# First three tiles' products over features without the token's factor, with their inputs loaded alternately

## The chip, the cores and the metric

The kernel runs on one core of one Trainium2 chip. The metric is the device time of one execution in microseconds (us); the median of three runs of the kernel before is 988.71. The core has five engines that work side by side, each through a queue of its own and in that queue's order: TensorE (PE) for matrix products into PSUM, VectorE (DVE), ScalarE (ACT), GpSimd (POOL), and SyncE (SP), which here only issues DMAs.

## The reference

One inference step of a decoder layer, over 512 prompt tokens and 8 samples of 8 tokens, 1024 features each. The start of it is what matters here:

```python
mod = jnp.matmul(cs, P['ada_w'][l]) + P['ada_b'][l]          # cs = silu(c)
sh1, sc1, g1, sh2, sc2, g2 = split(mod, 6)
hn = rmsnorm(x, P['norm1_w'][l]) * (1.0 + sc1) + sh1
u = jnp.matmul(hn, P['w_in'][l])
z, xbc, dt_raw, q, k, v, o, ig, fg, xr, gr = jnp.split(u, ...)
xbc = silu(causal_conv(xbc, ...))
```

rmsnorm multiplies each token by one factor, 1/sqrt(mean(x*x) + eps), and each feature by a weight. The scale sc1 and the shift sh1 depend on the feature and on the group: one set for the prompt, one for each sample. Since the token's factor r is a number for each column, W(x * amp * r + sh) is (W(x * amp)) * r + W sh, with amp = weight * (1 + sc1). Behind the projection come three mixers (an SSD scan, an mLSTM, a gated recurrence), an output projection and an MLP.

## The kernel before

Features lie on the 128 partitions, tokens in the free dimension: x is eight tiles (k = 0 to 7) of 128 x 576, 512 prompt columns and 64 sample columns. A weight block is 128 outputs by 1024 inputs; there are 124 of them, and each product runs in three passes over split operands (high weight by high x, high by low, low by high), each pass in two halves of 288 columns (mm_k, lines 155 to 165). One block with its eight k is 48 matmuls. w_prep (lines 132 to 153) splits a block: ACT copies the high half into fp32r, DVE subtracts for the low half. Three raw blocks fit in SBUF at a time.

Two PSUM pairs (psg) rotate through the blocks, and four single banks (psm) serve everything else. A block's first matmul so waits until the block two before it has been read out.

start (lines 327 to 419) is written inside in_order, which makes every engine keep the order in which the code is written. It does, in this order:

- SP loads the eight x tiles, the small vectors (vec), then the adaLN weights in pairs (ada, q = 0 to 7, 1 MB each in four DMAs; a pair holds shift and scale of tile q) with the weight blocks between them.
- ACT and DVE square all x tiles, PE sums over features (sum_tokens), DVE and POOL make the token's factor (rstd_cols), PE and ACT spread it over the partitions (rstd_bcast: five transposes, two copies).
- For each k: ada_mm (PE, one pair's rows), ada_sel (PE selects, DVE adds the bias into modt), modulate (lines 285 to 302): DVE multiplies the prompt columns by amp and factor in place, POOL does the 64 sample columns in three small steps, ACT adds the shift into the high half hnh, DVE subtracts for the low half hnl, POOL subtracts for the samples' low half and adds the shift to x itself (line 301, for the gates).
- Between them mm_k for the first three blocks (conv channels 8, 10 and 0), by the table TODO: products of tile k follow as soon as hn[k] is there. The third block sits in two psm banks.
- gates_mm: the gate columns from the modulated x, copied and selected. ev_gates and ev_conv read the results out; conv (lines 604 to 635) copies a block's PSUM with three ACT instructions into a row buffer, and ACT, DVE and POOL go on from there.

From there run (line 1269) goes through block 4 and up by unit, two slots of side work (gate_rows, the scans, the adaLN of later stages) per block, ordered by the framework's scheduler.

Of the kernel before, what the change touches and what calls it, by code (L numbers as in the profile page):

```python
# [67 lines left out]
class Kernel:  # L68
# [53 lines left out]
    def w_load(self, upto):  # L122
        while self.w_next_dma <= min(upto, NBLK - 1):
            b = self.w_next_dma
            t = self.T("wg") if b == 0 else self.wpool.tile([128, 1024], FT, name=self.name("raw"), tag="raw", bufs=RAW_BUFS)
            src = self.io["wg"] if b == 0 else self.io["w"][b - 1]
            n = src.shape[1]
            self.nc.sync.dma_start(t[:, :n], src)
            self.w_raw[b] = t[:, :n].rearrange("p (k m) -> p k m", k=8)
            self.w_next_dma += 1  # L130

# [153 lines left out]
    def modulate(self, x, rb, k):  # L285

        nc = self.nc
        amp = self.rpool.tile([128, 9], FT, name=self.name("amp"), tag="amp", bufs=3)
        sc, sh = self.mod("sc1", k), self.mod("sh1", k)
        nc.vector.tensor_scalar(amp, sc, 1.0, self.v("nw1")[:, k:k + 1], op0=OP.add, op1=OP.mult)  # L290
        p, s = x[:, :TP], x[:, TP:].rearrange("p (b t) -> p b t", b=NB)
        nc.vector.scalar_tensor_tensor(p, p, amp[:, 0:1], rb[:, :TP], op0=OP.mult, op1=OP.mult)
        nc.gpsimd.tensor_tensor(x[:, TP:], x[:, TP:], rb[:, TP:], op=OP.mult)
        nc.gpsimd.tensor_tensor(s, s, amp[:, 1:, None].to_broadcast([128, NB, 8]), op=OP.mult)
        nc.gpsimd.tensor_tensor(s, s, sh[:, 1:, None].to_broadcast([128, NB, 8]), op=OP.add)
        hi, lo = self.T("hnh", FR), self.T("hnl", FR)
        nc.scalar.activation(hi[:, :TP], p, AF.Identity, bias=sh[:, 0:1])
        nc.scalar.activation(hi[:, TP:], x[:, TP:], AF.Copy)
        nc.vector.scalar_tensor_tensor(lo[:, :TP], p, sh[:, 0:1], hi[:, :TP].bitcast(FT), op0=OP.add, op1=OP.subtract)
        nc.gpsimd.tensor_tensor(lo[:, TP:], x[:, TP:], hi[:, TP:].bitcast(FT), op=OP.subtract)  # L300
        nc.gpsimd.tensor_scalar(p, p, sh[:, 0:1], None, op0=OP.add)
        return hi, lo

# [23 lines left out]
    def start(self):  # L327
# [6 lines left out]
        with self.in_order():  # L334
            x = [self.T("x") for _ in range(KT)]
            for k in range(KT):
                nc.sync.dma_start(x[k], io["x"][:, k])
# [10 lines left out]

            def load(q):
                ada[q] = [self.T("ada") for _ in range(4)]  # L350
                for i in range(4):
                    nc.sync.dma_start(ada[q][i][:, :512], io["ada"][q, :, i * 512:(i + 1) * 512])

            for q in range(PAIR_AT):
                load(q)
                self.w_load(W_AT.get(q, 0))
            ms = self.P("ms")
            self.warm(WARM[0])
            for k in range(0, KT, 2):
                sa, sb = self.R()[:, :NT], self.R()[:, :NT]  # L360
                nc.scalar.activation(sa, x[k], AF.Square)
                if k:
                    nc.vector.tensor_tensor(sb, x[k + 1], x[k + 1], op=OP.mult)
                else:
                    nc.scalar.activation(sb, x[k + 1], AF.Square)
                nc.vector.tensor_tensor(sb, sa, sb, op=OP.add)
                self.sum_tokens(sb, ms, k == 0, k == KT - 2)
                if k < KT - 2:
                    self.warm(WARM[1])
# [3 lines left out]
            r = self.rstd_cols(ms, 1.0 / D, EPS)  # L373
            rows = {}

            def ada_mm(q):
                t = ada.pop(q)
                rows[q] = self.ada_mm(lambda k: t[k // 2][:, (k % 2) * 256:(k % 2 + 1) * 256])

            ada_mm(0)  # L380
            self.w_prep(0)
            for q in range(PAIR_AT, KT):
                if q == VEC_AT:
                    nc.sync.dma_start(self.vec[:, NV1:], io["vec"][:, NV1:])
                load(q)
                self.w_load(W_AT.get(q, 0))
            self.w_load(4)
            self.start_dma = self.last()
            rb = self.rstd_bcast(r)
            self.warm(WARM[2])  # L390
            self.ada_sel(0, rows[0])
            self.hn = [None] * KT
            self.hn[0] = self.modulate(x[0], rb, 0)
            self.w_prep(1)
            self.warm(WARM[3])
            ada_mm(1)
            self.ada_sel(1, rows[1])
            ada_mm(2)
            pgs = [self.PG(), self.PG(), PairTile(banks=[self.P("g"), self.P("g")])]
            for k in range(KT):  # L400
                if k + 1 < KT:
                    self.hn[k + 1] = self.modulate(x[k + 1], rb, k + 1)
                if k in PREP_AT:
                    self.w_prep(2 + PREP_AT.index(k))
                if k == KT - 1 and GATES_FIRST:
                    ps = self.gates_mm(x)
                for n, (i, kk) in enumerate(TODO.get(k, [(0, k), (1, k), (2, k)])):
                    self.mm_k(pgs[i], 1 + i, kk, self.hn[kk], kk == 0, kk == KT - 1)
                    if n == 0:
                        if k + 2 < KT:  # L410
                            self.ada_sel(k + 2, rows[k + 2])
                        if k + 3 < KT:
                            ada_mm(k + 3)
            if not GATES_FIRST:
                ps = self.gates_mm(x)
            self.ev_gates(ps)
            self.ev_conv(pgs[0], 8)
        self.ev_conv(pgs[1], 10)
        self.ev_conv(pgs[2], 0)

    def gates_mm(self, x):
# [10 lines left out]
        nc.scalar.activation(g[:, HALF:], ps[1][:, :HALF], AF.Copy)  # L432
        for h in range(2):
            nc.tensor.matmul(ps[h][:96, :HALF], self.v("selg"), g[:, h * HALF:(h + 1) * HALF], start=True, stop=True)
        return ps
# [168 lines left out]
    def conv(self, pg, dst, wcols, bias, state, out):  # L604

        nc = self.nc
        r = self.R()
        nc.gpsimd.memset(r[:, 0:3], 0.0)
        nc.gpsimd.tensor_copy(r[:, 515:603].rearrange("p (b t) -> p b t", b=NB)[:, :, 0:3], state)
        nc.scalar.activation(r[:, 3:3 + HALF], pg.h[0][:, :HALF], AF.Copy)  # L610
        n = TP - HALF
        nc.scalar.activation(r[:, 3 + HALF:515], pg.h[1][:, :n], AF.Copy)
        nc.scalar.activation(r[:, 515:603].rearrange("p (b t) -> p b t", b=NB)[:, :, 3:11],  # L613
                             pg.h[1][:, n:HALF].rearrange("p (b t) -> p b t", b=NB), AF.Copy)
# [22 lines left out]
    def ev_conv(self, pg, i):  # L637

        nc = self.nc
        if not hasattr(self, "cso"):  # L640
# [6 lines left out]
                      self.v("cst")[:, 24 * i:24 * i + 24].rearrange("p (b t) -> p b t", b=NB), self.cso[:, i])  # L647
# [621 lines left out]
    def run(self):  # L1269
# [9 lines left out]
        blk = 4  # L1279
# [6 lines left out]
        for i in range(1, 4):  # L1286
            inp(lambda pg: self.ev_conv(pg, i))
# [180 lines left out]
WARM = 14, 4, 4, 6  # L1468
PAIR_AT = 3
W_AT = {0: 1, 2: 2, 4: 3}  # L1470
VEC_AT = 7
PREP_AT = 1, 3, 6
# [165 lines left out]
```

## Time and profile before

| | us |
|---|---|
| runs of the kernel before, median (lowest to highest) | 988.71 (987.87 to 989.5) |
| the profiled execution | 991.71 |
| its span in the trace | 989.9 |
| PE busy | 959.0 |
| DVE busy | 579.1 |
| ACT busy | 400.4 |
| POOL busy | 134.9 |

The profiled execution lies 3.0 us above the median, and 1.8 us of it are outside the span. A row of the timeline gives start, duration, engine, line, operation, what it writes <- what it reads, and in brackets how long the engine sat idle before it and what released it. Equal neighbours are merged (x2). An fp32r matmul of 288 columns has one record, an fp32 one two. Tiles are named without their buffer numbers; g is a block's PSUM, hnh and hnl the halves of the modulated x, wh, wl and wt those of a weight block, adap and adas the adaLN rows and their selection.

### The profile page before, as it was taken

To read this page: it belongs to the slowest core of one execution; us is meant where nothing else is said; L and a number is where in the kernel's file an instruction comes from. 1 tells how busy PE (TensorE), PEld (TensorE's weight loads), DVE (VectorE), ACT (ScalarE), POOL (GpSimd) and SP (SyncE) were. 2 spreads that over 40 slices of the span, in tenths; PEclk is the share of its full clock that TensorE was granted. 3 is DMA by queue.
4 is the path that set the end of the run, shared out by engine and by line. 5 is a ranking of instruction groups with operands and counts; after the bars stand their busy time and mean duration, and the time that the engine had idled before them with its cause. 6 is when DMAs were issued, how large, how long until landed. Compare 5 with 4: busy or idle time off the path is not lost.

```text
span 989.9 us, 18136 instructions
## 1 busy us (share of the span) xinstructions
PE 959.0 (97%) x7370; PEld 904.9 (91%) x7370; DVE 579.1 (59%) x1206; ACT 400.4 (40%) x741; POOL 134.9 (14%) x194
## 2 busy tenths in 40 slices
PE   8899879999899999999999999999999999999996
PEld 4789868888788889998999999999999999999996
DVE  4669878687877586557444455533553355335544
ACT  3455734554656674436222243312431144114320
POOL 2811210420331222010000000000000000000032
PEclk9999989999999999999999999999999999999998
DMA  9722263764653424434333212222222222222202
GB/s 345 294 86 79 77 177 128 236 192 140 199 196 116 151 89 138 136 124 162 109 110 108 98 65 86 85 86 77 74 85 85 86 85 83 74 79 86 86 22 96
DMA packets 51218, 119.61 MB, mean 121 GB/s; under 512 B 6956, under 2 KB 17468, under 8 KB 51136
## 3 DMA queue, kind: packets, MB, share of 16 engines
q1 hardware_dynamic: 47024, 111.06, 33.3%
q10 hardware_dynamic: 3744, 6.85, 1.8%
q8 instruction: 58, 0.95, 0.4%
q0 software_dynamic: 368, 0.55, 0.2%
q14 instruction: 24, 0.20, 0.1%
HBM read 108.68 MB, written 9.76 MB: 120 GB/s over the span
## 4 chain that ended last, share of the span: by engine, by line
PE 84%; DVE 4%; ACT 3%; DMA 2%; issue 1%; POOL 0%; POOLq 0%; DVEq 0%; SPq 0%; ACTq 0%
PE g L163 73%; PE adap L217 1%; PE g L1363 1%; PE ps L733 1%; PE py L728 1%; DMA nmb<-scr_nm 1%; PE py L731 1%; DMA ada<-ada 1%; DMA cump<-scr_cum 0%; PE lg L1129 0%; PE xt L690 0%; PE adas L227 0%; DVE wl L151 0%; PE pu L828 0%; PE pn L970 0%
## 5 line engine op out<-in xcount | busy, mean ns | idle before, releaser
L150 ACT ACTIVATE wh<-raw 128x1024 fp32r<-128x1024 f32 x123 | 130.0, 1058 | 343.8 <-PE g L163 321.3
L151 DVE TENSOR_TENSOR wl<-raw,wh 128x1024 fp32r<-128x1024 f32 x123 | 151.3, 1231 | 43.2 <-ACT wh L150 37.8
L163 PE MATMUL g<-hnh,wh 128*128 128x288 f32 x688 | 155.6, 304 | 9.7 <-ACT r L613 5.2
L163 PE MATMUL g<-hnh,wl 128*128 128x288 f32 x688 | 153.0, 301 | 0.4 <-DVE wl L151 0.4
L163 PE MATMUL g<-hnl,wh 128*128 128x288 f32 x688 | 151.7, 300 | 0.0
L163 PEld LDWEIGHTS g<-hnh,wh 128*128 128x128 f32 x688 | 112.1, 191 | 19.1 <-ACT r L613 6.3
L163 PEld LDWEIGHTS g<-hnh,wl 128*128 128x128 f32 x688 | 112.4, 191 | 2.9 <-issue 1.5
L163 PEld LDWEIGHTS g<-hnl,wh 128*128 128x128 f32 x688 | 112.5, 191 | 1.9 <-issue 1.7
L163 PE MATMUL g<-h2h,wh 128*128 128x288 f32 (+1 forms) x512 | 111.2, 298 | 0.0
L163 PE MATMUL g<-h2l,wh 128*128 128x288 f32 (+1 forms) x512 | 111.1, 298 | 0.0
L163 PE MATMUL g<-h2h,wl 128*128 128x288 f32 (+1 forms) x512 | 110.4, 297 | 0.0
L163 PE MATMUL g<-hh,wl 128*128 128x288 f32 x480 | 102.7, 295 | 0.0
L163 PE MATMUL g<-hh,wh 128*128 128x288 f32 x480 | 102.7, 295 | 0.0
L163 PE MATMUL g<-hl,wh 128*128 128x288 f32 x480 | 102.6, 295 | 0.0
L306 DVE SCALAR_TENSOR_TENSOR xr<-g,modt,xr 128x288 f32<-128x288 f32 x38 | 19.7, 518 | 141.2 <-PE g L163 141.2
L163 PEld LDWEIGHTS g<-h2l,wh 128*128 128x128 f32 x512 | 83.7, 189 | 0.0
L163 PEld LDWEIGHTS g<-h2h,wl 128*128 128x128 f32 x512 | 83.6, 189 | 0.0
L163 PEld LDWEIGHTS g<-h2h,wh 128*128 128x128 f32 x512 | 83.0, 188 | 0.1
L163 PEld LDWEIGHTS g<-hh,wl 128*128 128x128 f32 x480 | 77.0, 188 | 0.0
L163 PEld LDWEIGHTS g<-hl,wh 128*128 128x128 f32 x480 | 76.9, 188 | 0.0
L163 PEld LDWEIGHTS g<-hh,wh 128*128 128x128 f32 x480 | 76.8, 188 | 0.0
L1405 POOL TENSOR_SCALAR xr<-xr,vec 128x576 f32<-128x576 f32 (+2 forms) x8 | 15.2, 1904 | 384.8 <-ACT sqa L1237 364.4
(398 smaller groups left out, 1523.7 us busy)
## 6 DMA issues: line engine op xcount, KB each, us to landing
raw<-w SPq DMA_DIRECT2D x124, 512.0 KB, 3.5
ada<-ada SPq DMA_DIRECT2D x32, 512.0 KB, 5.1
ada<-ada SPq DMA_DIRECT2D x32, 256.0 KB, 5.8
cumb<-scr_cum SPq DMA_DIRECT2D x16, 256.0 KB, 5.8
s<-s SPq DMA_DIRECT2D x16, 256.0 KB, 4.6
ssm_s<-s ACTq DMA_DIRECT2D x16, 256.0 KB, 4.2
x<-x SPq DMA_DIRECT2D x8, 288.0 KB, 5.2
xr<-x SPq DMA_DIRECT2D x8, 288.0 KB, 3.9
```

The costliest lines, as they stand in the source:

```text
L150: nc.scalar.activation(hi, raw, AF.Copy)
L151: nc.vector.tensor_tensor(lo, raw, hi.bitcast(FT), op=OP.subtract)
L163: self.nc.tensor.matmul(pg.h[h][:m, :e], w(k), xx[:, h * HALF:h * HALF + e], start=start and n == 0, stop=stop and n == 2)
L217: nc.tensor.matmul(ps[32 * j:32 * j + 32, :256], self.cs[:, k, :], ks(k), start=k < 4, stop=k >= 4)
L306: self.nc.vector.scalar_tensor_tensor(dst[:, :HALF], pg.h[0][:, :HALF], gate[:, 0:1], x[:, :HALF], op0=OP.mult, op1=OP.add)
L728: nc.tensor.matmul(o, xdt[:, h * 64:(h + 1) * 64], att[h // 4][:, hs], start=True, stop=not c)
L731: nc.tensor.matmul(o, S[:, h * 64:(h + 1) * 64], ce[h // 4][:, hs], start=False, stop=True)
L733: nc.tensor.matmul(pst, cb[:, 128:256], xend[:, :512], start=True, stop=True)
L1363: nc.tensor.matmul(pgs[i].h[p][:, :c.stop - c.start], w(k), xs[k][x][:, c], start=k == 0 and j == 0, stop=k == 7 and j == 2)
L1405: self.eng("fin").tensor_scalar(x, x, self.v("fnw")[:, o:o + 1], None, op0=OP.mult)
```

## The change

The first three blocks' products no longer take the modulated x, but x * amp, split into high and low halves (scale_only: hxh, hxl), which needs the adaLN pair of tile k but not the token's factor. Ten columns stand behind the 576 (nine shifts and a zero), so that the same product also yields W sh. late_rows then reads a block out of PSUM on DVE, multiplying by the factor (rb1) on the way, and adds W sh (ACT for the prompt, DVE for the samples). conv takes these rows in place of its three ACT copies. The modulated x is still made for all later blocks (modulate through whole), behind the eighth pair; for even k it now adds the shift on ACT into x itself and makes the halves of all 576 columns with one ACT copy and one DVE subtraction, for odd k it is as before. The fourth block (conv channel 1) moves into start, with the gates in its middle, and run begins at block 5.

The loads alternate: vec, then x0 q0 w1 x1 q1 w2 x2 q2 w3 x3 q3 x4 x5 q4 x6 x7 q5 w0 q6 v q7 w4 (q a pair, w a block, v the second half of vec). The warm matmuls (on zeros) are placed anew: 18, 3, 5, 2, 8 in place of 14, 4, 4, 4, 4, 6.

The core of the diff:

```diff
+    def scale_only(self, x, k):
+        amp = self.rpool.tile([128, 9], FT, name=self.name("amp1"), tag="amp1", bufs=KT)
+        nc.vector.tensor_scalar(amp, self.mod("sc1", k), 1.0, self.v("nw1")[:, k:k + 1], op0=OP.add, op1=OP.mult)
+        u = self.rpool.tile([128, TS + NSH], FT, name=self.name("xs"), tag="xs", bufs=2)
+        nc.gpsimd.tensor_copy(u[:, TS:TS + 9], self.mod("sh1", k))
+        nc.gpsimd.memset(u[:, TS + 9:], 0.0)
+        nc.vector.tensor_tensor(u[:, :TS]..., x[:, TP:]..., amp[:, 1:, None]..., op=OP.mult)
+        hi, lo = self.T("hxh", FR, True), self.T("hxl", FR, True)
+        nc.scalar.activation(hi[:, :TP], x[:, :TP], AF.Copy, scale=amp[:, 0:1])
+        nc.scalar.activation(hi[:, TP:n], u, AF.Copy)
+        nc.vector.scalar_tensor_tensor(lo[:, :TP], x[:, :TP], amp[:, 0:1], hi[:, :TP].bitcast(FT), ...)
+        nc.vector.tensor_tensor(lo[:, TP:n], u, hi[:, TP:n].bitcast(FT), op=OP.subtract)
+        return (hi, lo), amp
     def modulate(...)
+        if k % 2:
             nc.scalar.activation(hi[:, :TP], p, AF.Identity, bias=sh[:, 0:1])
             nc.scalar.activation(hi[:, TP:], x[:, TP:], AF.Copy)
             nc.vector.scalar_tensor_tensor(lo[:, :TP], p, sh[:, 0:1], hi[:, :TP].bitcast(FT), op0=OP.add, op1=OP.subtract)
             nc.gpsimd.tensor_tensor(lo[:, TP:], x[:, TP:], hi[:, TP:].bitcast(FT), op=OP.subtract)
             nc.gpsimd.tensor_scalar(p, p, sh[:, 0:1], None, op0=OP.add)
+        else:
+            nc.scalar.activation(p, p, AF.Identity, bias=sh[:, 0:1])
+            nc.scalar.activation(hi, x, AF.Copy)
+            nc.vector.tensor_tensor(lo, x, hi.bitcast(FT), op=OP.subtract)
+    def late_rows(self, pg):
+        nc.vector.tensor_copy(sh, pg.h[1][:, HALF:HALF + 9])
+        nc.vector.tensor_tensor(r[:, 3:3 + HALF], pg.h[0][:, :HALF], self.rb1[:, :HALF], op=OP.mult)
+        nc.vector.tensor_tensor(r[:, 3 + HALF:515], pg.h[1][:, :n], self.rb1[:, HALF:TP], op=OP.mult)
+        nc.vector.tensor_tensor(s, pg.h[1][:, n:HALF]..., self.rb1[:, TP:]..., op=OP.mult)
+        nc.scalar.activation(r[:, 3:515], r[:, 3:515], AF.Identity, bias=sh[:, 0:1])
+        nc.vector.tensor_tensor(s, s, sh[:, 1:, None]..., op=OP.add)
     def start(self):
...
+            ada_mm(0)
+            self.warm(WARM[1])
+            sel(0)
+            self.w_prep(1)
+            square(0)
+            self.warm(WARM[2])
+            mm(0, 0)
+            ada_mm(1)
...
+            mm(0, 3)
+            mm(1, 3)
+            mm(2, 3)
+            ada_mm(5)
+            ms = self.P("ms")
+            self.sum_tokens(sqa, ms, True, True)
+            r = self.rstd_cols(ms, 1.0 / D, EPS)
+            mm(0, 4)
+            sel(5)
+            mm(1, 4)
+            mm(2, 4)
+            ada_mm(6)
+            mm(0, 5)
+            sel(6)
+            self.rb1 = self.rstd_bcast(r)
+            mm(1, 5)
+            mm(2, 5)
+            ada_mm(7)
+            whole(0)
+            mm(0, 6)
+            sel(7)
+            self.w_prep(4)
+            mm(1, 6)
+            whole(1, 2)
+            mm(2, 6)
+            whole(3, 4)
+            for i in range(3):
+                mm(i, 7)
+            whole(5, 6, 7)
+            r0 = self.late_rows(pgs[0])
+            pg = self.PG()
+            for k in range(4):
+                self.mm_k(pg, 4, k, self.hn[k], k == 0, False)
+            ps, g = self.gates_mm(x)
+            r1 = self.late_rows(pgs[1])
+            self.w_load(8)
+            self.w_prep(5)
+            for k in range(4, KT):
+                self.mm_k(pg, 4, k, self.hn[k], False, k == KT - 1)
+                if k == 5:
+                    self.gates_sel(ps, g)
             self.ev_gates(ps)
-            self.ev_conv(pgs[0], 8)
-        self.ev_conv(pgs[1], 10)
-        self.ev_conv(pgs[2], 0)
+        self.ev_conv(pgs[0], 8, r0)
+        self.ev_conv(pgs[1], 10, r1)
+        self.ev_conv(pgs[2], 0, self.late_rows(pgs[2]))
+        self.ev_conv(pg, 1)
```

What it does to the queues shows best on DVE around the last adaLN pairs. Before, in the turn of k = 6 and 7 (x_89 and x_90): the selection's bias, the factor, the multiplication in place and the subtraction for each tile, then the low halves of weight blocks 4, 5 and 6, and the gates' copy.

```order
L228 TENSOR_TENSOR modt<-adas_536,vec 128x18
L290 TENSOR_SCALAR amp_569<-modt,vec 128x9
L292 SCALAR_TENSOR_TENSOR x_89<-x_89,amp_569,rb_279 128x512
L299 SCALAR_TENSOR_TENSOR hnl_576<-x_89,modt,hnh_575 128x512
L228 TENSOR_TENSOR modt<-adas_588,vec 128x18
L290 TENSOR_SCALAR amp_610<-modt,vec 128x9
L292 SCALAR_TENSOR_TENSOR x_90<-x_90,amp_610,rb_279 128x512
L299 SCALAR_TENSOR_TENSOR hnl_617<-x_90,modt,hnh_616 128x512
L151 TENSOR_TENSOR wl_624<-raw_270,wh_623 128x1024
L151 TENSOR_TENSOR wl_765<-raw_756,wh_764 128x1024
L151 TENSOR_TENSOR wl_769<-raw_758,wh_768 128x1024
L431 COPY gs_693<-gp_675 128x288
```

Now, behind the eighth pair's selection (modt of adas_613), its factor and scale_only, the same engine has the low half of block 4 and then the modulations one after the other; the rows below are the last three of these and the first block's way out of PSUM (g_204).

```order
L312 SCALAR_TENSOR_TENSOR x_88<-x_88,amp_112_508,rb_572 128x512
L320 SCALAR_TENSOR_TENSOR hnl_708<-x_88,modt,hnh_707 128x512
L312 SCALAR_TENSOR_TENSOR x_89<-x_89,amp_119_553,rb_572 128x512
L326 TENSOR_TENSOR hnl_719<-x_89,hnh_718 128x576
L312 SCALAR_TENSOR_TENSOR x_90<-x_90,amp_131_617,rb_572 128x512
L320 SCALAR_TENSOR_TENSOR hnl_728<-x_90,modt,hnh_727 128x512
L334 COPY shw_735<-g_204 128x9
L337 TENSOR_TENSOR r_734<-g_204,rb_572 128x288
L338 TENSOR_TENSOR r_734<-g_204,rb_572 128x224
L339 TENSOR_TENSOR r_734<-g_204,rb_572 128x8x8
```

The modulations stood one by one between the pairs' selections; now seven of them stand in a row behind the last one, ahead of the reading of g_204. On PE, the end of the third block was followed by the gates, and block 4 (g_755) came behind them:

```order
L163 MATMUL g_343<-hnh_616,wt_485 128x288
L163 MATMUL g_344<-hnh_616,wt_485 128x288
L428 MATMUL gp_675<-x_83,wg_114 32x288
L428 MATMUL gp_675<-x_84,wg_114 32x288
L428 MATMUL gp_675<-x_85,wg_114 32x288
```

Now the third block's last product (g_398, g_399) is followed at once by block 4 (g_742) on the modulated tiles, and the gates come behind its fourth k.

```order
L165 MATMUL g_398<-hxh_623,wt_351 128x288
L165 MATMUL g_399<-hxh_623,wt_351 128x298
L165 MATMUL g_742<-hnh_602,wh_629 128x288 x2
L165 MATMUL g_742<-hnl_603,wh_629 128x288 x2
L165 MATMUL g_742<-hnh_602,wl_630 128x288 x2
L165 MATMUL g_742<-hnh_643,wh_629 128x288 x2
```

g_742 uses the PSUM pair of g_204, so its first matmul stands behind the reading of g_204 by L334 to L339 on DVE.

More of the change, by code (lines that the diff above doesn't have):

```diff
@@ L347, in start @@
             ada = {}
[L349 to L357, printed above, removed]
-            self.warm(WARM[0])
[L359 to L369, printed above, removed]
+            for what, i in LOADS:
+                if what == "x":
+                    nc.sync.dma_start(x[i], io["x"][:, i])
+                elif what == "q":
+                    ada[i] = [self.T("ada") for _ in range(4)]
+                    for j in range(4):
+                        nc.sync.dma_start(ada[i][j][:, :512], io["ada"][i, :, j * 512:(j + 1) * 512])
+                elif what == "w":
+                    self.w_dma(i)
+                else:
+                    nc.sync.dma_start(self.vec[:, NV1:], io["vec"][:, NV1:])
+            self.w_next_dma = 5
+            self.start_dma = self.last()
+            self.w_prep(0)
+            self.warm(WARM[0])
             th = self.rpool.tile([128, 8, 32], FT, name="cth", tag="r")
@@ L372, in start @@
             nc.vector.scalar_tensor_tensor(self.cs, th, 1.0, ct, op0=OP.add, op1=OP.mult)
-            r = self.rstd_cols(ms, 1.0 / D, EPS)
[L374 to L413, printed above, removed]
@@ L414, in start, with ada_mm, sel @@
-            if not GATES_FIRST:
-                ps = self.gates_mm(x)
+            rows, amps, early = {}, {}, {}
+            sqa = self.T("sqa")[:, :NT]
+            def ada_mm(q):
+                if q < KT:
+                    t = ada.pop(q)
+                    rows[q] = self.ada_mm(lambda k: t[k // 2][:, (k % 2) * 256:(k % 2 + 1) * 256])
+            def sel(q):
+                if q < KT:
+                    self.ada_sel(q, rows.pop(q))
+                    early[q], amps[q] = self.scale_only(x[q], q)
@@ new lines, in whole @@
+            def whole(*ks):
+                for k in ks:
+                    self.hn[k] = self.modulate(x[k], self.rb1, amps[k], k)
+            ada_mm(0)
[6 more added lines that the diff above has]
+            ada_mm(1)
+            self.warm(WARM[3])
+            square(1)
+            sel(1)
+            self.w_prep(2)
+            self.warm(WARM[4])
+            mm(0, 1)
+            ada_mm(2)
@@ L1284, in inp @@
             blk += 1
-        for i in range(1, 4):
+        for i in range(2, 4):
             inp(lambda pg: self.ev_conv(pg, i))
```

113 lines of the change are left out of this document (77 added, 36 removed).

## The prediction

> **What bounds the kernel now.** The page comes first.
>
> ```profile
> span 989.9 us, 18136 instructions
> PE 959.0 (97%) x7370; PEld 904.9 (91%) x7370; DVE 579.1 (59%) x1206; ACT 400.4 (40%) x741; POOL 134.9 (14%) x194
> ```
>
> TensorE (PE) is busy for 97% of the span, so an idle microsecond of PE is a microsecond of the kernel unless a later wait swallows it. The change touches the first 70 us only, so the second view is the table by windows (columns: stretch; its sum; PE, PEld, DVE, ACT and POOL busy; granted clock; DMA share; GB/s).
>
> ```profile
> 0.00:5.00 5.00, 3.79 (x11) 1.44 (x12) 0.34 (x3) 2.73 (x4) 0.29 (x5) 1.00 0.62 180
> 5.00:10.00 5.00, 4.12 (x28) 2.72 (x26) 3.26 (x5) 1.49 (x3) 0.00 (x0) 1.00 1.00 365
> ...
> 45.00:55.00 10.00, 10.00 (x78) 10.00 (x77) 5.07 (x7) 4.73 (x7) 5.72 (x12) 1.00 0.16 55
> 61.00:69.00 8.00, 7.92 (x48) 7.92 (x49) 5.54 (x8) 3.17 (x7) 0.87 (x6) 0.79 0.01 2
> 69.00:100.00 31.00, 31.00 (x236) 31.00 (x236) 28.64 (x44) 18.60 (x35) 5.42 (x18) 1.00 0.25 85
> ```
>
> DMA runs flat out from 5 us. From 45 to 55 PE is full while DVE is half busy: here modulation hides behind products. From 69 to 100 PE is full and DVE nearly so. Third, PE's own rows at the borders of this stretch (start, duration, in us).
>
> ```profile
> 23.97 0.53 PE L163 MATMUL g<-hnh,wh 128*128 128x288 f32 x2
> ...
> 55.50 2.15 PE L428 MATMUL gp<-x,wg 128*32 128x288 f32 x32
> 57.77 1.21 PE L434 MATMUL gp<-gs,vec 128*96 128x288 f32 x4
> 61.08 0.54 PE L163 MATMUL g<-hnh,wh 128*128 128x288 f32 x2 [2.10 <-ACT r L613]
> ...
> 62.78 0.68 PE L163 MATMUL g<-hnh,wl 128*128 128x288 f32 x2
> ...
> 69.07 0.43 PE L163 MATMUL g<-hnh,wh 128*128 128x288 f32 x2
> ```
>
> The first three tiles run from 23.97 to 55.5, the gates behind them, weight block 4 from 61.08 and block 5 from 69.07. The start of block 5 is my yardstick: from there on both kernels have the same products left.
>
> **What the change moves.** It starts products before the norm is known, and puts the whole modulation of all eight tiles behind the eighth adaLN pair. What one turn of modulation costs, one turn of the present loop shows.
>
> ```profile
> 40.71 0.75 DVE L292 SCALAR_TENSOR_TENSOR x<-x,amp,rb 128x512 f32<-128x512 f32 x1
> ...
> 41.49 0.72 ACT L297 ACTIVATE hnh<-x,modt 128x512 fp32r<-128x512 f32 x1 [1.09 <-DVE x L292]
> 41.50 0.32 POOL L293 TENSOR_TENSOR x<-x,rb 128x64 f32<-128x64 f32 x1
> ...
> 41.89 0.30 POOL L294 TENSOR_TENSOR x<-x,amp 128x64 f32<-128x64 f32 x1
> ...
> 42.25 0.87 DVE L299 SCALAR_TENSOR_TENSOR hnl<-x,modt,hnh 128x512 fp32r<-128x512 f32 x1 [0.79 <-ACT hnh L297]
> ...
> 42.60 0.26 ACT L298 ACTIVATE hnh<-x 128x64 fp32r<-128x64 f32 x1 [0.38 <-POOL x L295]
> ...
> 43.28 1.57 POOL L301 TENSOR_SCALAR x<-x,modt 128x512 f32<-128x512 f32 x1
> ...
> 44.02 0.75 DVE L292 SCALAR_TENSOR_TENSOR x<-x,amp,rb 128x512 f32<-128x512 f32 x1
> ...
> 44.81 0.32 POOL L293 TENSOR_TENSOR x<-x,rb 128x64 f32<-128x64 f32 x1
> ```
>
> DVE multiplies (40.71), waits 0.79 for ACT, subtracts (0.75 to 0.87; I take 0.75). POOL's small sample steps stand 0.39 apart, and its turn is 3.31 (41.50 to 44.81). Prices of PE's pieces, and of the others:
>
> ```profile
> 39.82 0.53 PE L163 MATMUL g<-hnh,wh 128*128 128x288 f32 x2
> ...
> 41.51 0.51 PE L227 MATMUL adas<-vec,adarow 128*128 128x9 f32 x4
> ...
> 41.95 1.07 PE L217 MATMUL adap<-ada,cs 128*32 128x256 f32 x16
> ...
> 42.95 0.53 PE L163 MATMUL g<-hnh,wh 128*128 128x288 f32 x2
> ```
>
> ```profile
> 5.16 0.76 DVE L366 TENSOR_TENSOR r<-r,r 128x576 f32<-128x576 f32 x1 [3.99 <-ACT r L365]
> ...
> 8.02 0.68 ACT L361 ACTIVATE r<-x 128x576 f32<-128x576 f32 x1 [1.46 <-DVE r L363]
> 8.93 1.26 PE L269 MATMUL ms<-ones,r 128*128 128x1 f32 x10 [0.73 <-DVE r L366]
> ...
> 15.74 1.12 PE L277 MATMUL ba<-vec,col 128*128 128x128 f32 x4
> ...
> 16.89 0.60 ACT L281 ACTIVATE rb<-ba 128x512 f32<-128x512 f32 x1 [0.74 <-PE ba L277]
> 17.39 0.22 ACT L282 ACTIVATE rb<-bb 128x64 f32<-128x64 f32 x1
> ...
> 19.04 0.23 DVE L290 TENSOR_SCALAR amp<-modt,vec 128x9 f32<-128x9 f32 x1
> 21.07 1.04 ACT L150 ACTIVATE wh<-raw 128x1024 fp32r<-128x1024 f32 x1
> 24.17 0.38 ACT L219 ACTIVATE adarow<-adap 128x256 f32<-128x256 f32 x1 [1.79 <-PE adap L217]
> 30.76 1.23 DVE L151 TENSOR_TENSOR wl<-raw,wh 128x1024 fp32r<-128x1024 f32 x1 [1.42 <-ACT wh L150]
> 39.01 2.52 POOL L301 TENSOR_SCALAR x<-x,modt 128x512 f32<-128x512 f32 x1
> 57.26 0.46 DVE L431 COPY gs<-gp 128x288 f32<-128x288 f32 x1 [0.83 <-PE gp L428]
> ```
>
> From 39.82 to 41.95 are two "products" (six matmuls each: one tile, one k) and one selection: I take 0.78 and 0.57; with the ten extra columns in half of the matmuls 0.79. A pair's rows (ada_mm) take 1.0 (41.95 to 42.95).
>
> *1. The early start.* The first pair stands behind 1.71 MB (vec, x0, q0) in the queue; 0.9 MB have moved by 5 us, the rest at 365 GB/s gives 7.2, and I add 1.0 for the last packets: ada_mm(0) at 8.3. Row copy (0.38, and 0.2 that I take for the handover from PE), selection, factor (0.2+0.23), high copy (0.72 and 0.26) and weight copy (1.04), in that order, give the first product at 13.2, 10.8 earlier than now. Pairs 1 and 2 each wait for this chain again (the kernel fills with warm matmuls), so ada_mm(2) starts at about 20.7. From there PE has 16 products (12.6), six ada_mm (6.0), five selections (2.9), the sums (1.0) and the broadcast (1.4): 23.9, and some 3.0 of waits for the copies of pair 2, row 4 and the squares. ada_mm(7) ends at 47.6, and, with the last six products, selection 7 and 1.4 of waiting for the copies of tile 7, the three tiles end at 54.8: **0.7 earlier** than now's 55.5 only, because the early chain waits and PE does the pairs as before.
>
> *2. The norm's factor* is broadcast from 43.6; two groups of transposes on PE (1.4) and two copies (0.60, 0.22) put it at 46.0 (now 17.6). DVE's first whole modulation starts there, but ACT stands in its queue before ada_mm(7)'s row (47.8 to 48.2), then adds (0.72) and copies (0.68) for x0, so DVE subtracts until 50.4. Behind it come pair 7's factor, ACT's 0.72 and 0.75 + 0.2 of subtraction (52.7), then block 4's low half behind ACT's 1.04 (1.23, until 54.2).
>
> *3. The run of seven modulations*, k = 1 to 7, now has DVE to itself and PE has nothing left beside it. k = 1: 0.75 + 0.72 + 0.75 with two handovers of 0.05: 2.3, so 56.5. Then pairs of an even and an odd k. The even k's ACT copy spans all 576 columns and so waits for POOL's three sample steps, which stand in POOL's queue behind the odd k's 1.57 addition, which waits for DVE's subtraction. One pair: 1.57 + (0.39 + 0.39 + 0.31) + 0.68 + 0.76 on the even side, 0.75 + 0.72 + 0.75 on the odd, five handovers of 0.05: 6.6. Three pairs: 19.8, until 76.3. late_rows reads tile 0 out of PSUM on DVE (0.07, 0.46, and 0.40 and 0.2 scaled from it): 77.4. Block 4's first matmul waits for exactly this, because its PSUM pair is tile 0's. **PE idles from 54.8 to 77.4, 22.6 us**; everything behind that matmul on PE, gates and block 5 included, is queued behind it.
>
> The Trainium skill's "SBUF — State Buffer", section "Who interferes with whom", says that a DVE instruction with two SBUF inputs and a GpSimd instruction that reads SBUF exclude each other for the whole instruction. By that rule POOL's 1.57 would wait out DVE's next multiply three times, 2.3 more, and the time would be 1010 rather than 1008. This trace is split: L292 at 44.02 ran its 0.75 inside L301's unlengthened 1.57 at 43.28, while L301 at 39.01 took 2.52. I keep 1.57 and give the long one to the range.
>
> *4. Block 4.* Now 69.07 - 61.08 = 8.0, with a stretch at half clock after the gap (0.68 rows; clock 0.79 in the window). After a gap nine times as long I take the same. Inside it now lie the gates (55.50 to 57.7: 2.2) and their selection (0.6), which the old kernel had done before. Block 5 starts at 77.4 + 10.8 = 88.2: **19.1 later**.
>
> *5. Behind it.* The lists are the same from here. DVE enters with more undone: two weight halves (2 x 1.23), the third tile's rows (1.1) and part of a convolution, up to 6; but the gate rows' chain also moves one block later and takes load from DVE there. I take 0, and 0 to 6 for the range. The three tiles' ACT copies vanish, ACT being 18.60 of 31 busy: nothing. The squares, now off ACT and DVE's path, also nothing; the cover is PE's 23.9 of queued work.
>
> The profiled execution took 991.71 with a span of 989.9; plus 19.1 it is 1010.8. It lies 3.0 above the median of 988.71, so the forecast for the median is 988.71 + 19.1 = **1007.8**.
>
> **Rivals.**
>
> *The modulations hide (faster).* If DVE released tile 0's PSUM before the tiles end at 54.8, block 4 would follow at once and, with no gap, at full clock (6.4 + 2.8): block 5 at 64.0, 5.1 earlier, 983.6. The point is 58.3 for that release (69.07 - 10.8). Against it: DVE's own work behind the factor is 16 x 0.75 + 1.6 (pair 7) + 1.23 + 1.13 = 16.0, so from 46.0 it ends at 62.0 without one wait. The factor would have to come 3.7 earlier too. For it: only that my early chain is long. 7%.
>
> *POOL does not gate.* If the sample steps get ahead of the addition, an even k costs 0.75 + 0.72 + 0.68 + 0.76 and handovers, and the three pairs lose 3.7 in all: 1004.1. For it: POOL's spans are rough. Against: ACT's 0.38 wait for POOL at 42.60. 18%.
>
> *Everything collides.* POOL's 2.52 in place of 1.57 (three times, 2.9) and a DVE backlog of 6: 1016.7. 17%.
>
> *Later waits swallow part.* PE's waits behind 61 us are led by these two:
>
> ```profile
> PE py L728 <- DVE att L710: 6.2, 2, 5.8
> PE g L163 <- ACT r L613: 5.2, 3, 2.1
> ```
>
> If both came from a DVE that has now caught up in the gap, 11.4 would return: 996.4. Against: DVE spent the gap on modulation, not on what follows. 8%; with another 3% that more returns, down to no change.
>
> **How the numbers follow.** The forecast keeps 47% (1004 to 1013). The range runs from 996, the swallowed case, to 1017, the collision; what it leaves out is the first rival and the 3%, and what lies beyond its ends. A measurement tells about 0.2% (2 us) from no change. Faster 0.07, within 0.03, slower 0.90: only the first rival, and a chain that errs by 20 us, ends at or under today's time.
>
> **What would show it.** Right: a PE gap of about 20 us behind the third tile's last product, released by DVE's late_rows; in it DVE alternating with ACT and POOL at 6.6 per two k; first product near 13; block 5 near 88. Wrong: the factor's broadcast well before 43, or block 4 following within a few us of the third tile; or a gap as told but PE's waits behind 100 us gone.

## The result

The changed kernel takes **1030.5 us** (median of 4 runs, 1028.92 to 1033.9); the kernel before takes 988.78 beside it (987.87 to 989.5). The ratio is **1.0407** (95% interval 1.0373 to 1.0441): 41.7 us slower. The forecast was 1007.8, with a range of 996 to 1017. Times below are medians of the runs in the fast state, which leaves out one run of the modulations one ahead (1749.96 us at a mean clock of 0.85).

The page of the changed kernel (span; then busy time, share and instructions of each engine). The profiled execution took 1033.9.

```profile
span 1032.1 us, 18158 instructions
PE 972.3 (94%) x7339; PEld 911.9 (88%) x7340; DVE 593.2 (57%) x1245; ACT 409.8 (40%) x754; POOL 134.3 (13%) x202
```

TensorE (PE) is busy for 13 us more and idle for 29 us more. Its rows at the borders of the start, in the order of the code: first product, last product of the third tile, block 4, gates, blocks 5, 6 and 7 (a block is 48 products, so the rows can be counted off).

```profile
13.28 0.53 PE L165 MATMUL g<-hxh,wh 128*128 128x288 f32 x2 [1.34 <-ACT wh L152]
...
54.01 0.44 PE L165 MATMUL g<-hxh,wt 128*128 128x288 f32 x2
...
77.91 0.82 PE L165 MATMUL g<-hnh,wh 128*128 128x288 f32 x2 [23.46 <-DVE r L339]
...
83.90 2.15 PE L526 MATMUL gp<-x,wg 128*32 128x288 f32 x32
...
90.22 0.43 PE L165 MATMUL g<-hnh,wh 128*128 128x288 f32 x2
...
100.85 0.85 PE L165 MATMUL g<-hnh,wh 128*128 128x288 f32 x2 [4.13 <-ACT r L714]
...
108.86 0.43 PE L165 MATMUL g<-hnh,wh 128*128 128x288 f32 x2
```

The gap is there, 23.46 us long and ended by late_rows' last multiplication out of PSUM (L339). Block 5 starts 21.15 later than before's 69.07. Block 6, which waited for nothing before, waits 4.13. The same stretches by windows (columns as in the prediction):

```profile
54.45:77.90 23.45, 0.00 (x0) 0.03 (x1) 10.81 (x18) 7.75 (x15) 15.00 (x28) 0.54 0.07 23
77.90:90.20 12.30, 12.29 (x84) 10.63 (x85) 4.61 (x12) 5.05 (x7) 1.70 (x3) 0.76 0.00 0
90.20:100.85 10.65, 6.52 (x50) 6.29 (x48) 10.55 (x19) 6.49 (x12) 3.12 (x5) 1.00 0.50 160
```

In the gap every engine waits for another: VectorE (DVE) works 10.81 of 23.45 us, ScalarE (ACT) 7.75, GpSimd (POOL) 15.00. Block 4 and the gates then run at a mean clock of 0.76. Behind them it is VectorE that is full (10.55 of 10.65).

How much later does each weight block start? Counting the products of all blocks in the traces (us, against the profiled execution of before; the last three columns belong to the experiments):

| block | before | after | two rounds more | gates late | rounds late |
|---|---|---|---|---|---|
| 5 | 69.07 | +21.15 | +19.45 | -6.25 | -2.27 |
| 7 | 81.77 | +27.09 | +26.56 | -6.25 | -2.27 |
| 14 | 149.72 | +18.38 | +26.84 | -16.89 | -10.47 |
| 17 | 183.39 | +14.11 | +26.82 | -21.13 | -14.72 |
| 18 | 198.67 | +26.99 | +25.32 | -8.78 | -2.28 |
| 20 | 219.57 | +39.44 | +25.69 | +3.99 | +9.04 |
| 24 | 280.42 | +41.23 | +25.83 | +4.20 | +7.83 |
| 40 | 416.97 | +41.26 | +25.94 | +4.31 | +8.21 |

So half of the loss comes behind block 5, and it is complete by block 24. From there on the two traces run in step, as the norm's sums show (before, then after: 41.2 apart):

```profile
435.96 1.15 PE L269 MATMUL ms<-ones,zsq 128*128 128x1 f32 x10
```

```profile
477.17 1.16 PE L271 MATMUL ms<-ones,zsq 128*128 128x1 f32 x10
```

The column "after" first falls, to +14, and then jumps: other work has changed places with the blocks. Two windows each: from block 5 to block 24, and the 42 us from the first pc on. There the SSD's sample stage (pc, pu, pin) and the first mLSTM head (pn and its pu) have their products; the expectations below call them the first mLSTM head's for short. Before:

```profile
69.07:280.42 211.35, 198.39 (x1610) 174.54 (x1608) 172.26 (x425) 116.81 (x264) 46.32 (x73) 0.98 0.50 157
173.09:215.09 42.00, 40.84 (x325) 34.80 (x317) 31.25 (x88) 23.71 (x62) 14.87 (x18) 1.00 0.76 243
```

After:

```profile
90.22:321.65 231.43, 211.41 (x1609) 183.72 (x1608) 182.42 (x438) 118.21 (x266) 53.21 (x75) 0.92 0.47 148
213.56:255.56 42.00, 36.13 (x211) 28.32 (x211) 27.21 (x74) 18.40 (x52) 12.57 (x12) 0.72 0.59 178
```

As many products take 231.43 in place of 211.35: 20.1 more. 13.0 of it is busy time (211.41 - 198.39, the clock 0.92 in place of 0.98), 7.1 is waiting, 4.1 of that block 6's. In the second pair of windows 211 matmuls are done where 325 were, at a clock of 0.72. PE's rows there say why; before, with the weight blocks' products left out as "...":

```profile
173.09 1.04 PE L821 MATMUL pc<-s,xbc 128*32 128x512 f32 x8
...
176.16 0.62 PE L828 MATMUL pu<-xst,bst 96*128 96x512 f32 x2
...
179.66 0.97 PE L838 MATMUL pin<-vec,cc 128*128 128x32 f32 x8
```

After, with nothing left out up to the first pn:

```profile
213.56 1.07 PE L922 MATMUL pc<-s,xbc 128*32 128x512 f32 x8
216.21 0.47 PE L929 MATMUL pu<-xst,bst 96*128 96x512 f32 x1 [1.58 <-ACT xst L902]
216.82 0.73 PE L929 MATMUL pu<-xst,bst 96*128 96x512 f32 x1 [0.15 <-ACT v L1047]
218.54 1.92 PE L939 MATMUL pin<-vec,cc 128*128 128x32 f32 x8 [0.99 <-ACT cc L925]
220.27 1.21 PE L1071 MATMUL pn<-v,nmb 128*128 128x130 f32 x4
...
225.66 0.68 PE L165 MATMUL g<-hnh,wh 128*128 128x288 f32 x2
```

Before, products of weight blocks fill PE from 174.1 to 176.2 and from 176.8 to 179.7, while ScalarE and VectorE prepare pu and pin. After, the steps stand side by side: PE waits, the clock halves (pin 1.92 against 0.97), and no block runs for 12 us.

### The profile page after: what moved, and what is told of

It reads as the page before. It is cut to its first block, busy times and chain, and to the rows that moved or that the text cites. A ratio compares the mean times of both kernels' runs of the same rounds, so it can differ in the third digit from the quotient of the medians.

```text
span 1032.1 us, 18158 instructions
## 1 busy us (share of the span) xinstructions
PE 972.3 (94%) x7339; PEld 911.9 (88%) x7340; DVE 593.2 (57%) x1245; ACT 409.8 (40%) x754; POOL 134.3 (13%) x202
## 4 chain that ended last, share of the span: by engine, by line
PE 80%; DVE 7%; ACT 5%; DMA 3%; issue 2%; POOL 1%; SPq 1%; POOLq 0%; DVEq 0%; ACTq 0%
PE g L165 69%; PE adap L219 2%; DVE wl L153 1%; DMA ada<-ada 1%; PE g L1464 1%; PE ps L834 1%; PE py L829 1%; DVE att L807 1%; ACT wh L152 1%; PE adas L229 1%; DMA nmb<-scr_nm 1%; DMA cumb<-scr_cum 1%; POOL x L322 1%; ACT xst L902 1%; DMA cumf<-scr_cum 1%
## 5 line engine op out<-in xcount | busy, mean ns | idle before, releaser
L165 PE MATMUL g<-hnh,wh 128*128 128x288 f32 x656 | 150.8, 309 | 33.0 <-DVE r L339 23.5
L165 PE MATMUL g<-hnh,wl 128*128 128x288 f32 x656 | 147.3, 304 | 0.0
L165 PEld LDWEIGHTS g<-hnh,wh 128*128 128x128 f32 x656 | 109.3, 195 | 40.5 <-issue 28.3
L165 PE MATMUL g<-hnl,wh 128*128 128x288 f32 x656 | 144.9, 302 | 0.0
L165 PEld LDWEIGHTS g<-hnl,wh 128*128 128x128 f32 x656 | 109.2, 194 | 0.6 <-issue 0.4
L165 PEld LDWEIGHTS g<-hnh,wl 128*128 128x128 f32 x656 | 108.9, 194 | 1.0 <-issue 0.4
```

Of the source, the lines that this page charges most:

```text
L165: self.nc.tensor.matmul(pg.h[h][:m, :e], w(k), xx[:, h * HALF:h * HALF + e], start=start and n == 0, stop=stop and n == 2)
```

## The experiments

Behind the start the side work is emitted by generators; one round (slot) takes the next piece of each. Theory A: the loss has two parts, the front (gap, clock, block 6's wait) and the order behind the start. The gate rows are handed to the rounds by ev_gates, which the change moves behind block 4, so the rows, and the SSD and mLSTM work that waits for them, are emitted one block later; the scheduler then lays the SSD's sample products and the first mLSTM head's side by side. Theory B: what is lost behind block 5 is VectorE's and ScalarE's backlog out of the gap. Ratios are to the kernel before, run beside each.

**Two rounds more.** The order alone undone in the changed kernel:

```
         self.ev_conv(pg, 1)
+        self.slot()
+        self.slot()
```

> The changed kernel with two extra rounds of the generators right behind the start, so that the gate rows are handed out as early, counted in weight blocks, as in the kernel before; on TensorE the order of everything from the gate rows' first transpose on is then that of the kernel before, and the start is unchanged. Theory A (order): block 7 starts 27.1 us later than before because of the front, and the other 14.2 of the 41.3 come from the order behind it, which puts the first mLSTM head's products side by side with no weight blocks between them. Then block 7 stays 26 to 30 late (the rows' chain now has less cover, which may add a wait of up to 5), the half-clock stretches near 217 and 241 us go, and the time is 1014 to 1021. Theory B (backlog): the 14.2 come from VectorE and ScalarE work left over from the gap. Then the time stays at 1028 or more.

Measured: 1019.12, ratio 1.0281 (1.0256 to 1.0306): by the ratios 12.5 us less than the change, as A has it. Block 7 is still 26.56 late and nothing is added behind it (table). That the order is back can be counted: in the 25 blocks from block 5 on the traces hold 835 matmuls that belong to no block. Here 830 of them stand behind as many block products as in the kernel before; in the changed kernel 467 do. The window from pc is as before:

```profile
199.92:241.92 42.00, 42.00 (x333) 35.91 (x326) 32.71 (x92) 24.08 (x63) 14.93 (x18) 1.00 0.77 245
```

**Gates late.** In the kernel before: block 4's loop with the gates in its middle, as the change has it. The edit also moves the first tile's evaluation (ev_conv) ahead of block 4 and the gates.

> The kernel before with one edit: weight block 4 is run ahead of the gates' evaluation, with the gates' products in its middle, as the changed kernel does; no early products, no late rows, no gap. Theory A (order): block 5 starts within 3 us of 69.07, and the products of the first mLSTM head again stand side by side, so the time is 1000 to 1006. Theory B (backlog from the gap): there is no gap here, so the time is 987 to 993.

Measured: 998.37, ratio 1.0071 (1.0044 to 1.0098), between the two. Both theories missed the start and the time: block 5 comes 6.25 earlier. ScalarE's rows for tile 0, here and before:

```profile
50.79 0.41 ACT L617 ACTIVATE r<-g 128x288 f32<-128x288 f32 x1 [1.84 <-PE g L163]
```

```profile
60.25 0.41 ACT L610 ACTIVATE r<-g 128x288 f32<-128x288 f32 x1
```

Before, they stand in ScalarE's queue behind the gates' copies, and block 4 waits for them; here they stand ahead of the gates, and they are done before block 4 starts at 52.97. (Some 2.3 of the 6.25 are not the edit's: with an untouched start block 5 came that much earlier in another execution, last column of the table.) Behind it 10.45 are lost, from -6.25 at block 7 to +4.20 at block 24, where A had put 14.2 to the order.

**The modulations one ahead.** In the changed kernel VectorE multiplies k+1 before it subtracts k, and all k take the even form:

```
+        mul(1)
+        for k in range(1, KT):
+            if k + 1 < KT:
+                mul(k + 1)
...
+            nc.scalar.activation(p, p, AF.Identity, bias=self.mod("sh1", k)[:, 0:1])
+            nc.scalar.activation(hi, x[k], AF.Copy)
+            nc.vector.tensor_tensor(lo, x[k], hi.bitcast(FT), op=OP.subtract)
```

> The changed kernel with the seven late modulations in another order of the same kind of steps: VectorE multiplies k+1 ahead of subtracting k, and all k take the form with two ScalarE copies over the tile, without GpSimd's addition over 512 columns. Theory A: a pair of modulations takes 7.03 us because VectorE waits in order for ScalarE, and ScalarE for GpSimd's sample steps behind its 2.0 us addition. Per k then remain 1.4 to 1.6 us (VectorE 0.75 + 0.76, ScalarE 0.72 + 0.68), the run of seven ends near 67, block 4 starts at 67 to 70 and the time is 1019 to 1024 (what lies behind is unchanged). Rival: the ports or ScalarE hold VectorE anyway; then a pair stays above 5.5, block 4 starts behind 73, and the time is 1026 or more.

Measured: 1016.89, ratio 1.0260 (1.0234 to 1.0285). VectorE's rows stand 1.5 apart per k (multiply, subtract, multiply), and the gap halves; block 4's start and the time come out a little under what A had:

```profile
58.28 0.76 DVE L349 TENSOR_TENSOR hnl<-x,hnh 128x576 fp32r<-128x576 f32 x1
58.95 0.79 DVE L336 SCALAR_TENSOR_TENSOR x<-x,amp,rb 128x512 f32<-128x512 f32 x1
59.77 0.76 DVE L349 TENSOR_TENSOR hnl<-x,hnh 128x576 fp32r<-128x576 f32 x1
```

```profile
66.23 0.82 PE L165 MATMUL g<-hnh,wh 128*128 128x288 f32 x2 [12.28 <-DVE r L362]
```

**Even form only.** The changed kernel with "if False" for "if k % 2": no GpSimd addition over 512 columns, the old order.

> The changed kernel with every late modulation in the form of the even k (two ScalarE copies, no GpSimd addition over 512 columns), in the same order, so VectorE still subtracts k before it multiplies k+1. Theory A (VectorE in order): per k remain 0.75 + 0.72 + 0.68 + 0.8 and handovers of 0.2, 3.15, against 7.03 for a pair and 2.3 for the first odd k: block 4 starts 0.5 to 2 us earlier, and the time is 1028 to 1030. Rival (GpSimd's addition is what holds the run): per k under 2.4, block 4 starts 5 or more earlier, and the time is under 1025.

Measured: 1028.66, ratio 1.0372 (1.0339 to 1.0404). Per k VectorE now takes 3.0, and block 4 starts at 74.68, 3.2 earlier: more than A's 0.5 to 2, less than the rival's 5. The time is A's.

```profile
54.95 0.76 DVE L326 TENSOR_TENSOR hnl<-x,hnh 128x576 fp32r<-128x576 f32 x1 [1.56 <-ACT hnh L325]
...
57.97 0.76 DVE L326 TENSOR_TENSOR hnl<-x,hnh 128x576 fp32r<-128x576 f32 x1 [1.55 <-ACT hnh L325]
```

So GpSimd's addition is worth 0.5 per k (7.03 / 2 - 3.0), and VectorE's waiting in order for ScalarE the other 1.5.

**PE kept warm.** 100 idle products ahead of block 4: self.warm(100) behind the first late_rows.

> The changed kernel with 100 idle bf16 products of 0.22 us (22 us) on TensorE in the gap, ahead of block 4. Theory A: they end before 77.9, so block 4 starts where it did; the granted clock is then 1.00 there, block 4 and the gates take some 9.4 instead of 12.3, and the time is 1026 to 1029. Rival: the half clock costs nothing because VectorE and ScalarE bound that stretch; the time stays within 1 us of 1030.5. Another: the products run at half clock too and end behind 77.9, then the time is over 1031.

Measured: 1026.5, ratio 1.0360 (1.0328 to 1.0391), 4 us under the change, though the intervals overlap. The products ended early; behind the wait of 1.91 that was left the clock was half again for 3.41 us, so block 4 and the gates took 11.2, where A had 9.4:

```profile
53.67 21.76 PE L542 MATMUL warm<-wz 128*128 128x512 bf16 x100
77.34 0.51 PE L165 MATMUL g<-hnh,wh 128*128 128x288 f32 x2 [1.91 <-DVE r L339]
```

**Both edits at the gap.** One ahead, and the first late_rows ahead of the run:

```
+            r0 = self.late_rows(pgs[0])
             self.run_ahead(x, amps)
...
-            r0 = self.late_rows(pgs[0])
```

> The changed kernel with the seven late modulations multiplied one ahead, as in the run above of that edit, and with the first tile's late rows, which free block 4's PSUM, ahead of the run in place of behind it. The order behind the start is as in the changed kernel. Theory A: TensorE then takes block 4 tile by tile beside the modulations, the gap of 11 us that was left falls to waits of 1 to 2 per k, block 5 starts 6 to 8 earlier than in that run (70.5 to 73), and the time is 1007 to 1013. Rival: the wait only moves to block 5 or 6, which wait for row buffers and PSUM behind a busy VectorE; then the time stays above 1014.

Measured: 1010.61, ratio 1.0195 (1.0161 to 1.0228). Block 4 runs k by k beside the modulations and the gap is gone, so what made the gap is settled. Block 6 waits longer, though:

```profile
57.98 0.54 PE L165 MATMUL g<-hnh,wh 128*128 128x288 f32 x2 [1.37 <-ACT hnh L348]
...
71.63 0.43 PE L165 MATMUL g<-hnh,wh 128*128 128x288 f32 x2
...
83.05 0.61 PE L165 MATMUL g<-hnh,wh 128*128 128x288 f32 x1 [4.93 <-ACT r L735]
```

**Both, and two rounds** (right behind ev_gates):

> The changed kernel with the modulations multiplied one ahead, the first late rows ahead of the run (both as in the run of these two edits: block 7 9.7 us late, the whole 19.2 late), and two rounds of the generators right behind the start. The first mLSTM head's products then stand mostly apart. Theory A (order): of the 9.5 that were lost behind block 7 most go, block 7 stays 8 to 11 late, and the time is 997 to 1004. Rival: the loss behind block 7 is VectorE's backlog; the time stays at 1007 or more.

Measured: 1000.52, ratio 1.0091 (1.0055 to 1.0126), 10 us less than without the rounds: A again. Block 6 waits 9.21 here, and block 7 is 12.4 late, where A had 8 to 11.

**Gates first.** The changed kernel with the gates' products ahead of block 4, so that their values come earlier, at the same place in the emission:

> The changed kernel with the gates' products ahead of block 4 in place of in its middle, their selection behind k = 1 of it: the gate rows' values are ready some 6 us earlier, but they are handed to the generator rounds no earlier, and the first mLSTM head's products stand side by side as in the changed kernel. Theory A (order): block 5 starts where it did within 1.5 us, and the time stays at 1028 to 1032. Rival (the loss comes from the rows being computed late): the time falls to 1024 or less.

Measured: 1028.57, ratio 1.0388 (1.0327 to 1.0449), as A has it, though the interval's lower end, some 1024, touches the rival. Earlier values alone bring little.

**Six row buffers.** The changed kernel with bufs=6 in place of 4 for the tiles of tag "r":

> The changed kernel with six row buffers in place of four. Theory A: block 6 waits 4.13 us for ScalarE to copy block 4 out of PSUM, and that copy waits for a row buffer, since the three late tiles hold theirs until VectorE has convolved them (the row before it ends at 99.93, the copy starts at 100.02). With free buffers the copies follow block 4's last product, the wait goes, and the half-clock stretch behind it too (1.7): block 7 is 21 to 23 us late in place of 27.1 and the time is 1023 to 1027. Rival: VectorE and ScalarE are behind in their own order, and block 6 or 7 waits for them as long; the time stays at 1029 or more.

Measured: 1032.07, ratio 1.0418 (1.0366 to 1.0470). Block 6's wait falls to 1.69 and block 7 is 22.93 late, as A said, but the time does not fall: at block 14 it is 19.4 late (the change: 18.4). A had taken PE's wait there for time lost; it is given back.

**Backlog.** Six buffers, and two of three multiply-adds left out of the convolutions of the start's four tiles:

> The changed kernel with six row buffers, as in the run above of that edit (1.0418 of before), and with two of the three multiply-adds of VectorE left out in the convolutions of the four tiles of the start (8 x 0.84, 6.7 us of VectorE's work between 87 and 110 us); left out of the result too. Theory C: between the gates and the first SSD unit VectorE is busy for 93 to 99% and sets the pace, so that waits of TensorE alone (block 6's, which six buffers shorten by 2.4) are given back later, and VectorE's work is not: the SSD and the mLSTM products come 4 to 7 us earlier and the time is 1.035 to 1.038 of before. Rival: what comes behind is set by the order and the DMAs between, not by VectorE; the time stays within 0.15% of 1.0418.

Measured: 1019.42, ratio 1.0267 (1.0217 to 1.0317): by the ratios 15 us less for 6.7 us of VectorE's work, which neither C nor its rival had. The gain stands before block 17 (2.63 late there, with six buffers alone 15.14); the loss between blocks 17 and 20 stays. It looked like theory B. The same omission in two more kernels, with four buffers:

> The kernel before with two of three multiply-adds left out of the convolutions of the same four tiles (left out of the result too), as a control. If the gap made VectorE's work the limit behind it, the kernel before, whose VectorE does that work earlier beside full TensorE, gains 5 us at most (0.995 to 1.001). Rival: VectorE's work there is the limit in both kernels; then it gains 8 to 15 us as the changed one did (0.992 or less), and that gain says nothing on the change.

Measured: 981.41, ratio 0.9875 (0.9827 to 0.9922). The kernel before, which has no gap, gains 12.4 by it, so a gain of this size is no sign of a backlog out of the gap. VectorE's work is not all that differs in this run: 602 of the 835 matmuls stand where they stood.

> The changed kernel with both edits: two rounds of the generators behind the start (alone 1.0281 of before) and two of three multiply-adds left out of the convolutions of the start's four tiles (with six row buffers 1.0267; left out of the result too). If the order behind the start and VectorE's backlog are two losses, they add up: 1.013 to 1.018 of before. Rival: they are the same loss seen twice; then it stays at 1.023 or more.

Measured: 1017.9, ratio 1.0248 (1.0219 to 1.0277). Beside the two rounds the omission brings only 3, as the rival has it: the two do not add up, and the order is laid anew here too (659 of 835 stand as with the rounds alone). These three runs thus neither separate VectorE's work from the order nor show B; B is answered by the next run, which has no gap. Why 6.7 us of work are worth 12 to 15 in two kernels stays open.

**Rounds late.** The order alone, in the kernel before, its start untouched:

```
-        self.active.append(self.gate_rows(v, ic))
+        self.rows_later = self.gate_rows(v, ic)
...
             inp(lambda pg: self.ev_conv(pg, i))
+            if i == 1:
+                self.active.append(self.rows_later)
```

> The kernel before, its start untouched, with the gate rows handed to the generator rounds one weight block later (behind block 4 in place of ahead of it), as the changed kernel does, and nothing else. The order of TensorE behind the start then has the first mLSTM head's products side by side as in the changed kernel. Theory A (order): block 5 starts at 69 as before, and the time is 1.010 to 1.014 of before, what the two rounds took off the changed kernel. Rival (the 12 us are bound to the late start, the order is a symptom): the time stays within 0.3% of before.

Measured: 1003.97, ratio **1.0145** (1.0111 to 1.0179), 14.3 us, with block 5 at 66.80. The profiled execution, with 999.16 the fastest of the six, shows 10.1 of it between blocks 5 and 24 (-2.27 to +7.83). 703 of the 835 matmuls stand as in the changed kernel, 442 as in the kernel before, and the window from pc looks like the changed kernel's:

```profile
184.69:226.69 42.00, 35.40 (x223) 27.95 (x223) 29.20 (x76) 18.75 (x52) 13.88 (x13) 0.80 0.57 178
```

That settles it: the order is one cause by itself, without any gap, and of about the size that the two rounds took off the changed kernel (12.5).

**Gates late, and two rounds.** Both in the kernel before:

> The kernel before with block 4 ahead of the gates' evaluation, as in the run above of that edit, and with two rounds of the generators right behind the start, so that the gate rows are handed out no later, counted in blocks, than before. In the run above block 5 started 6.25 us earlier than before and 10.3 were lost again between blocks 17 and 20, where the first mLSTM head's products stand side by side. Theory A (order): here they stand apart again (22 weight blocks' products between the first of them, 22 before the next), so the 6.25 stay: 982 to 987. Rival: the loss comes from the gates being evaluated later, whatever the order; then the time is 993 or more.

Measured: 987.29, ratio **0.9966** (0.9934 to 0.9998; 12 runs), by the ratios 10 us less than without the rounds, as A has it. Against the kernel before the gain is 3 us, and the interval ends just under 1. Block 4 fills the wait for the gates' copies, and the steps from pc stand apart again (window of 42 us: PE 41.40, clock 1.00).

```profile
165.35:207.35 42.00, 41.40 (x320) 34.47 (x313) 31.73 (x87) 23.30 (x60) 14.57 (x18) 1.00 0.73 242
```

> The kernel before with block 4 ahead of the gates and two rounds of the generators behind the start (0.9966 of before in the run above, where block 6 still waited 2.85 us for ScalarE's copies of block 4), and with six row buffers in place of four. If that wait is for a row buffer, it goes, and the time is 981 to 985 where before takes 989 to 991; if it is ScalarE's own order, the time stays at 985 to 988.

Measured: 987.39, ratio 0.9972 (0.9940 to 1.0005). Block 6's wait of 2.85 goes (block 6 at 72.74 in place of 74.73) and the time stays: by block 14 it is 6.88 early, the run without the six buffers 8.22.

## Why the prediction was half right

*1. Early start: right.* First product 13.28 (forecast 13.2), three tiles done at 54.45 (54.8). The terms named add up to 12.9 and 54.3, so 0.3 and 0.5 of the two forecasts have no term behind them. The early start is used up waiting for pairs, as said.

*2. The factor: right.* It stands at 45.8 (46.0), and VectorE is through with the weights' low half at 53.6 (54.2):

```profile
45.57 0.21 ACT L284 ACTIVATE rb<-bb 128x64 f32<-128x64 f32 x1
```

*3. The run of seven: right, the gap 4% short.* A pair took 7.03 (6.6), the gap 23.46 (22.6). One pair, and the last of the long additions, which meets no such multiply:

```profile
55.71 0.81 DVE L312 SCALAR_TENSOR_TENSOR x<-x,amp,rb 128x512 f32<-128x512 f32 x1
55.95 2.01 POOL L322 TENSOR_SCALAR x<-x,modt 128x512 f32<-128x512 f32 x1
...
58.70 0.29 POOL L315 TENSOR_TENSOR x<-x,modt 128x64 f32<-128x64 f32 x1
...
59.03 0.68 ACT L325 ACTIVATE hnh<-x 128x576 fp32r<-128x576 f32 x1 [1.76 <-POOL x L315]
...
59.74 0.89 DVE L326 TENSOR_TENSOR hnl<-x,hnh 128x576 fp32r<-128x576 f32 x1 [3.23 <-ACT hnh L325]
...
62.08 0.75 DVE L320 SCALAR_TENSOR_TENSOR hnl<-x,modt,hnh 128x512 fp32r<-128x512 f32 x1 [0.79 <-ACT hnh L318]
...
77.19 1.57 POOL L322 TENSOR_SCALAR x<-x,modt 128x512 f32<-128x512 f32 x1
```

The chain is the forecast's, link by link: GpSimd's addition, its sample steps, ScalarE's copy, VectorE. GpSimd's addition took 2.01 where I took 1.57, which is the 0.43 per pair. It overlaps VectorE's multiply, which still had 0.57 to run; the one at 77.19 took 1.57. The Trainium skill's "SBUF — State Buffer", section "Who interferes with whom", has such a pair exclude each other. 56.52 + 1.57 gives 58.09 against a measured end of 57.96, so these rows agree with it, at a smaller price than the 0.75 per pair that I had worked out for it. Where the addition starts first they do not: in the kernel before the multiply ran its 0.75 inside it (44.02 in 43.28 to 44.85, rows of the prediction).

*4. Block 4: mis-sized by 1.5.* 12.31 (10.8). I took the half clock to last as long as after before's short wait; it lasted from 77.91 to 83.8. (My gap was not nine but eleven times that wait, 22.6 against 2.10.) Block 5 thus came 21.15 later (19.1).

*5. "Behind it" is the step that failed.* It said "The lists are the same from here" and took 0, with 0 to 6 for the range; measured are 20.1. The sentence was wrong: the lists' members are the same, their order is not. I saw that the gate rows' chain moves one block later and counted it as relief for VectorE. What I did not ask is what the rounds emit in its place. That alone costs 14.3 in the kernel before, and undoing it returns 12.5 of the 41.7 (by the ratios). VectorE's backlog, which I did expect, shows as block 6's wait (4.13) and half-clock rows behind it, +5.9 by block 7, the upper end of my 6; six buffers took most of that wait away, and no time. In a sum: 21.15 up to block 5, 5.9 to block 7, 14.1 from there to block 24, where the order acts.

*The rivals.* "Everything collides" had GpSimd's long addition and the backlog right and the order missing. "POOL does not gate" is wrong as the change stands, and right in that GpSimd's addition is the smaller part: 0.5 per k against 1.5 for VectorE's waiting in order. "Later waits swallow part" went the other way: waits were added.

The range of 996 to 1017 came from steps 1 to 4 and a bound that knew of backlog alone. With the order kept, the changed kernel takes 1.0281 of before, 1016.5 at the forecast's 988.71: just inside that range, at its upper end.

## What to carry to other kernels

Where a scheduler or rounds of generators emit the work, moving one call across a block moves everything that waits for it: compare the order of the whole remainder before pricing only the edited stretch. A modulation that alternates between engines costs the sum of its steps per tile unless the next tile's first step is issued ahead of the last one's last; off the path that sum is free, on it it was 23 us. A wait of one engine need not be worth its length: with six buffers two kernels lost PE waits of 2.4 and 2.9 us and gained nothing. That another engine was behind there is my reading (VectorE was busy for 10.55 of 10.65 us in the changed kernel); no run shows it by itself.

## What was not expected of the hardware

The half clock outlasts its cause. In the window from pc PE waited 1.58 and 0.99 us, and further on 1.89 and 0.78:

```profile
240.43 0.42 PE L1118 MATMUL pj<-ci,vec 128*32 128x130 f32 x4 [1.89 <-DVE s L935]
241.63 1.22 PE L1125 MATMUL pw<-vm,stk 96*128 96x512 f32 x2 [0.78 <-DVE s L935]
```

Behind the first wait of each pair it ran at half clock, for 10.24 and for 13.64 us, though it was busy for 9 tenths of both:

```profile
216.93:227.17 10.24, 9.25 (x36) 8.02 (x37) 6.85 (x12) 4.92 (x15) 3.54 (x4) 0.50 0.60 152
240.83:254.47 13.64, 12.39 (x51) 9.36 (x50) 8.74 (x32) 3.86 (x15) 0.00 (x0) 0.50 0.75 244
```

The Trainium skill's "TensorE: Matmul & The Clock Gate", Part 1, has full clock return after at least one busy window of about 3.4 us, sustained. By that figure, an estimate, the two stretches are three and four windows long. The two cost some 12 us, an estimate from half of their 23.88. In the kernel before two single waits of 1.55 between blocks (102.50 and 111.23) left the clock at 1.00. So in this trace a stretch of small products with several waits ran at half clock as a whole; what counts as busy there no run here shows.
